# Moving operands of the down product and of block T3 placed in the uppermost 32 KB of the on-chip memory

## The chip, the cores and the metric

The kernel runs on one core of a Trainium2 chip. A core has a matrix engine (TensorE, PE in the profile; its weight loads are listed apart as PEld), three elementwise engines (VectorE or DVE, ScalarE or ACT, GpSimd or POOL), and a queue that only issues transfers (SyncE, SP). They share an on-chip memory of 128 partitions. Addresses below are in KB from the start of a partition, as the tiles get them when the two programs are built; the memory reaches to 224 KB, so "uppermost 32 KB" means 192 to 224. Matrix products are summed in a second memory, PSUM. The metric is the time of one execution on the device, in microseconds (us).

## The reference

One decoder layer on x of 1024 positions by 1024 columns, float32. Two token mixers (windowed attention and a chunked spatial gate) are merged by two gates and added to x; then follows a gated MLP with a causal width-3 convolution over positions:

```
x = x + (sigmoid(g_a) * (y_att @ w_oa) + sigmoid(g_b) * (y_sgu @ w_ob)) @ w_out
z = rmsnorm(x) @ w_up                    # 1024 x 1024 times 1024 x 5632
zc = conv_b + sum over 3 taps of conv_w[tap] * shifted z
x = x + (silu(gate half of zc) * value half) @ w_down     # 2816 x 1024
```

The change touches the gates (g_a, g_b are 2048 of the 3840 columns of a combined input projection), the up product and the down product.

## The kernel before

**Products.** Every float32 operand is split into a high and a low part (`copy_hi`, L75, on ScalarE, then a subtraction on GpSimd or VectorE), and a product is three matmuls: high by high, high by low, low by high. A matmul takes 128x128 weights and a moving operand of at most 512 columns, and each comes with its own weight load.

**Seven products for eight.** Gates, up product and down product use a scheme with seven block products on half-size blocks. On the side that moves, the blocks are named B11, T1, B21, B22, T2, T3, T4; on the weight side A11, A12, S1 to S4, A22. In the gates and the up product `Blocks.prod` (L914) issues 12 matmuls of 512 columns for one block product (4 blocks of the contraction, 3 each), so a pair of output tiles is 84 matmuls; there are 8 gate pairs (`first_gate_pair`, `gate_pair`) and 22 up pairs (`first_pair`, `fast_pair`). In both stages T3 is always multiplied with the weights s3h and s3l.

**The down product** (`mlp`) runs seven steps M1, M2, M6, M7, M4, M5, M3. Each is cut into six groups of 24 matmuls (the last: 12), 42 groups in all, numbered g = 0 to 41. The matmuls are those of L1595: weights ah, al, moving operands bh, bl. For a group `loads` fetches b (the stored activations) and the rows of w_down from DRAM, and `prep` makes ah, al, bh, bl in rings of four slots each: `copy_hi` for ah and bh on ScalarE, L1570 for al and bl (bl on GpSimd for g < 4, else on VectorE). `prep(g + 3)` is issued behind the matmuls of group g. b is held in three buffers.

**Order.** The order on the PE is written by hand. All transfers go through SP's queue in program order, and each engine does its instructions in order; waits come from the buffers: a tile placed where another one lay waits for the last use of that one. The last up pair still has its convolution, gating and stores to do when the down product begins: `q.gated()` and `q.stores()` stand behind group 1. `stores` writes five blocks to DRAM (`put`, L1338), two of them from the temporary tiles tt (L605). Only behind it is the pool of these temporaries closed and its space given to others.

**Homes of the tiles before.** Gates: T3 at 208 to 224, s3h and s3l at 203.5 to 207.5, other temporaries around them. Up product: T3 at 171.5 to 187.5, weights s3h and s3l at 165.5 to 169.5, and the pairs' temporaries (x1, x7, u2, tv, tg, tt) above, at 187.5 to 221.5. Down product: bh at 23.5 to 39.5, bl at 71.5 to 87.5, ah at 7.5 to 23.5, al at 87.5 to 103.5. Only two other sets of moving operands lie in the uppermost 32 KB for more than a few matmuls: wvB (the second half of an input weight, 208 to 225) and the attention keys.

**The twins wv and wvB.** In the projection for the spatial gate the same activations x are weights (at 23.5 to 103.5) for two moving operands of the same shape, 256 columns each: wv at 39.5 to 55.5 and wvB at 208 to 225. They take turns in one stretch, 192 matmuls each (L79 to L81).

Of the kernel before, what the change touches and what calls it, by code (L numbers as in the profile page):

```python
# [10 lines left out]
F = mybir.dt.float32  # L11
R = mybir.dt.float32r
# [29 lines left out]
def body(ctx, tc, nc, a):  # L42
# [7 lines left out]
    def nm(s):  # L50
        uid[0] += 1
        return f"{s}_{uid[0]}"

    def Y(s, dt=R, shape=None):
        return big.tile(shape or [128, 4, 1024], dt, tag="Y", name=nm(s), bufs=7)

    def U(s, dt=R, shape=None):

        return big.tile(shape or [128, 4, 1024], dt, tag="U", name=nm(s))
# [14 lines left out]
    def copy_hi(dst, src, scale=1.0):  # L74
        return nc.scalar.activation(dst, src, AF.Copy, scale=scale)  # L75
# [528 lines left out]
    def sub(eng, out, x, y, op=ALU.subtract):  # L604
        eng.tensor_tensor(out, x, y, op=op)  # L605
        return out
# [195 lines left out]
    pools = {"dr": dr}  # L802
# [31 lines left out]
    class Left:  # L834
# [54 lines left out]
                                                for x in "hl"))  # L889

        def split_s3(self):
            self.split(("S3",), self.s3, *(pools["wx"].tile([128, 4, 128], R, tag="s3" + x, name=nm("s3" + x))
                                           for x in "hl"))

        def split_r(self, n=0):
# [41 lines left out]
    def sums_load():  # L937

        i = sums["load"]
        if i < NPAIR:  # L940
            x = pools["ls"].tile([128, 3, 4, 128], F, tag="ls", name=nm("ls"), bufs=2)
            nc.sync.dma_start(x[:, 0], a["wup"][2 * i][:, 0:4])
            nc.sync.dma_start(x[:, 1:3], a["wup"][2 * i + 1].rearrange("p (b k) m -> p b k m", b=2))
            sums[i] = x
            sums["load"] += 1
# [25 lines left out]

    def gates_open():
        pools["ls_cm"] = tc.tile_pool(name="ls", bufs=1)
        pools["ls"] = pools["ls_cm"].__enter__()
        pools["gp_cm"] = tc.tile_pool(name="gp", bufs=1)
        gp = pools["gp"] = pools["wx"] = pools["gp_cm"].__enter__()
        pools["AX"] = gp.tile([128, 2, 1024], R, name="gax")
        sums_load()
# [174 lines left out]
    def open_out():  # L1153
        pools["mg_cm"].__exit__(None, None, None)
        pools["ls_cm"].__exit__(None, None, None)
        s3_cm.__exit__(None, None, None)
        pools["wx"] = ctx.enter_context(tc.tile_pool(name="wx", bufs=1, reuse_waits="tile"))
        pools["ex"] = ctx.enter_context(tc.tile_pool(name="ex", bufs=1, reuse_waits="tile"))
        pools["fp_cm"] = tc.tile_pool(name="fp", bufs=1, reuse_waits="tile")
        fp = pools["fp"] = pools["fp_cm"].__enter__()  # L1160
        for n in ("B11", "T1", "B21", "B22"):
            comb[n] = Y(n, R, [128, 2, 4, 512])
        comb["T3"] = pools["ex"].tile([128, 2, 4, 512], R, tag="T3", name="T3")
        pools["raw2"], pools["raw4"] = (fp.tile([128, 4, 512], F, name=n) for n in ("T2f", "T4f"))
        pools["sq2"] = fp.tile([128, 1024], F, name="sq2")
        dr = pools["dr"]
        pools["x2"] = [dr.tile([128, 1024], F, tag=f"x2_{d}", name=f"x2_{d}") for d in range(8)]
        for n in ("B11", "B21", "B22", "T1", "T2", "T3", "T4"):
            pools["d" + n] = [dr.tile([128, 512], F, tag=f"{n}_{i}", name=f"{n}_{i}") for i in range(HK)]
        out_load(D_ORDER[0])  # L1170
        psum["P"].insert(0, psum["P"].pop())
# [6 lines left out]
    def out_load(d):  # L1178
        acs[d] = pools["fp"].tile([128, 1024], F, tag="ac", name=nm("ac"), bufs=2)
        nc.sync.dma_start(acs[d], a["xw"][d, :, 257:1281])  # L1180
# [5 lines left out]
    def out_tile(i):  # L1186
        d = D_ORDER[i]

        def main(w):
            if i == 0:  # L1190
                open_out()
# [73 lines left out]
    late = {}  # L1265
# [219 lines left out]
        q.prod(q.g1, "S4", "B22", more=True)  # L1485
        return q

    SUM_AT = (2, 4, 5, 7, 8, 10)
    GR = [(k, min(k + 2, HK)) for k in range(0, HK, 2)]
    STEPS = ("M1", "M2", "M6", "M7", "M4", "M5", "M3")  # L1490
    RHS = {"M1": "B11", "M2": "B21", "M6": "T2", "M7": "T3", "M4": "T4", "M5": "T1", "M3": "B22"}
# [2 lines left out]
    def mlp():  # L1494
        groups = [(s, k0, k1) for s in STEPS for k0, k1 in GR]
        blk, ring = {}, {}
        zz = []

        def block(n, k0, k1):

            if k0 < 8:
                if n not in blk:
                    blk[n] = Y(n, F, [128, 8, 512])
                return blk[n][:, k0:k1, :]
            if not zz:
                zz.append(pools["ex"].tile([128, 8, 512], F, tag="T3", name="zz"))
            b = 3 * ("A11", "S2").index(n) - 8
            return zz[0][:, b + k0:b + k1, :]

        def slot(n, dt, cnt):  # L1510

            if n not in ring:
                y = pools["yd"].tile([128, 8, 512], F, name="rs") if n == "rs" else Y(n, dt, [128, 8, 512])
                ring[n] = [y, 0]
            y, i = ring[n]
            ring[n][1] += 1
            return y[:, 2 * (i % 4):2 * (i % 4) + cnt, :]
# [37 lines left out]
        def prep(g):  # L1555
            s, k0, k1 = groups[g]
            n = k1 - k0
            x, b = raw_.pop(g)
            if s == "M6":
                x = block("S2", k0, k1)  # L1560
            elif s in ("M7", "M3"):
                sub(nc.vector, x, x, block("S2", k0, k1))
            elif s == "M5":
                x = block("A11", k0, k1)
                sub(nc.vector, x, x, block("S2", k0, k1), ALU.add)
            out = []
            for t, nh, nl, eng in ((x, "ah", "al", nc.vector), (b, "bh", "bl", nc.gpsimd if g < 4 else nc.vector)):
                h, l = slot(nh, R, n), slot(nl, R, n)
                copy_hi(h, t)
                eng.tensor_tensor(l, t, h.bitcast(F), op=ALU.subtract)  # L1570
                out += [h, l]
            ops_[g] = out
# [26 lines left out]
        rs = {}  # L1599

        def res(n, t):

            r, c = int(n[1]) - 1, int(n[2]) - 1
            rs[n] = t
            for d in range(4):
                nc.sync.dma_start(t[:, d, :], pools["x2"][4 * r + d][:, 512 * c:512 * c + 512])
# [5 lines left out]
        def plus(n, d, p, last=False):  # L1612

            t = rs[n][:, d, :]
            nc.vector.scalar_tensor_tensor(t, p, 0.5, t, op0=ALU.mult, op1=ALU.add)
            if last:
                put(n, d, t)

        def done(s):
            for d in range(4):  # L1620
                if s == "M1":
                    nc.scalar.copy(Yb[d], X[d])
                if s == "M2":
                    plus("C11", d, Yb[d], True)
                if s == "M6":
                    plus("C21", d, X[d])
                if s == "M7":
                    nc.scalar.activation(rs["x7"][:, d, :], Yb[d], AF.Copy, scale=0.5)
                if s == "M4":
                    plus("C21", d, Yb[d], True)  # L1630
                if s == "M5":
                    plus("C22", d, X[d], True)
                if s == "M3":
                    plus("C12", d, X[d], True)
            if s == "M1":
                y = U("res", F, [128, 2, 4, 512])
                res("C11", y[:, 0])
                res("C21", y[:, 1])
                rs["y"] = y
            if s == "M2":  # L1640
                y = pools["yd"].tile([128, 2, 4, 512], F, name="res2")
                res("C22", y[:, 0])
                rs["x7"] = y[:, 1]
            if s == "M7":
                nc.vector.tensor_tensor(rs["C22"], rs["C22"], rs["x7"], op=ALU.add)
            if s == "M4":
                res("C12", rs["y"][:, 0])
# [18 lines left out]
        for g in range(len(groups)):  # L1666
            mms(g)
            s, k0, k1 = groups[g]
            while n_load < min(g + 6, len(groups)):
                loads(n_load)  # L1670
                n_load += 1
            if g in SUM_AT:
                sum_loads(*GR[SUM_AT.index(g)])
            if k1 == HK:
                done(s)
            if g == 0:
                q.tap_v()
                q.last_sum()
                q.conv_v()
                prep(2)  # L1680
                q.tap_g()
                q.conv_g()
            if g == 1:
                q.gated()
                q.stores()
                pools["ft_cm"].__exit__(None, None, None)
                pools["yd"] = ctx.enter_context(tc.tile_pool(name="yd", bufs=1, reuse_waits="tile"))
            if g + 3 < len(groups):
                prep(g + 3)
            if g - 2 in SUM_AT:  # L1690
                sums2(*GR[SUM_AT.index(g - 2)])
            if g == 0:
                q.tanh()
# [91 lines left out]
```

## Time and profile before

| | us |
|---|---|
| median of 3 runs | 1218.7 (1217.72 to 1218.85) |
| span of the profiled execution, first to last instruction | 1218.1 |
| PE busy in it | 1195.9 |
| DVE busy | 893.3 |
| ACT busy | 542.1 |
| POOL busy | 568.0 |

The page gives the profiled execution as its span of 1218.1; what lies around the span is the 0.6 between it and the median. A matmul's end is modelled in the trace, and neighbours overlap, so a mean duration of 389 ns says little: the pace of the PE is read from the distance of the starts.

### The profile page before, as it was taken

The numbers are of one execution on the slowest core, as the hardware profiler recorded it, in microseconds if no ns is written. First come the engines' busy times: TensorE is split into PE (matmuls) and PEld (weight loads), VectorE is DVE, ScalarE is ACT, GpSimd is POOL, SyncE is SP. The second block draws the span as 40 slices with busy tenths as digits, with TensorE's granted clock in tenths as the row PEclk, the third lists the DMA queues.
The fourth block names the chain that finished last, engine by engine and source line by source line (L and its number), as shares of the span: only waits on it lengthen the run. The fifth ranks groups of instructions, "written<-read, shape, count | busy, mean of one in ns | idle before, by whom it ended". The sixth has DMA issues, their size and how long they took to land.

```text
span 1218.1 us, 15838 instructions
## 1 busy us (share of the span) xinstructions
PE 1195.9 (98%) x5866; PEld 1004.7 (82%) x5866; DVE 893.3 (73%) x1033; ACT 542.1 (45%) x830; POOL 568.0 (47%) x358
## 2 busy tenths in 40 slices
PE   9999999889999999999999999999999999999998
PEld 8888889868887888888788888888888888888886
DVE  7788866874455665577798788887888888775674
ACT  8555566733434322223444444444444445424331
POOL 2466584278766522334756657566575642000000
PEclk9999999989999999999899999999999999999999
DMA  7010133125767897442223334233332347975471
GB/s 274 26 52 19 53 121 139 42 85 169 256 237 274 289 348 286 156 156 103 96 87 121 121 113 145 88 122 117 117 141 90 124 166 274 386 253 190 143 233 66
DMA packets 78989, 191.27 MB, mean 157 GB/s; under 512 B 8896, under 2 KB 9152, under 8 KB 78912
## 3 DMA queue, kind: packets, MB, share of 16 engines
q1 hardware_dynamic: 78912, 190.26, 44.3%
q8 instruction: 46, 0.75, 0.2%
q14 instruction: 31, 0.25, 0.1%
HBM read 139.63 MB, written 50.59 MB: 156 GB/s over the span
## 4 chain that ended last, share of the span: by engine, by line
PE 87%; DVE 6%; DMA 3%; ACT 2%; issue 1%; POOL 1%; SPq 0%; ACTq 0%; DVEq 0%
PE pz L914 42%; PE pd L1595 10%; PE pdy L1595 7%; PE px L81 2%; PE px L79 2%; PE po L79 2%; PE po L81 2%; PE po L80 2%; PE px L80 2%; DMA ls<-wup 2%; PE pv L498 1%; PE pu L81 1%; PE pu L79 1%; PE pu L80 1%; DVE T L750 1%; PE pq L79 1%
## 5 line engine op out<-in xcount | busy, mean ns | idle before, releaser
L914 PE MATMUL pz<-T,qh 128*128 128x512 f32 x464 | 142.8, 389 | 0.0
L879 POOL TENSOR_TENSOR pl<-lp,ph 128x1024 fp32r<-128x1024 f32 x30 | 73.6, 2455 | 85.0 <-ACT ph L75 84.9
L914 PE MATMUL pz<-B,ph 128*128 128x512 f32 x352 | 109.5, 392 | 0.0
L914 PEld LDWEIGHTS pz<-T,qh 128*128 128x128 f32 x464 | 87.2, 188 | 18.1
L914 PE MATMUL pz<-T,ql 128*128 128x512 f32 x232 | 90.3, 389 | 0.0
L96 POOL TENSOR_TENSOR wjl<-wj,wjh 128x512 fp32r<-128x512 f32 (+1 forms) x24 | 41.1, 1713 | 95.2 <-ACT wjh L75 95.2
L879 POOL TENSOR_TENSOR ql<-lq,qh 128x1024 fp32r<-128x1024 f32 x30 | 77.5, 2582 | 14.8 <-ACT qh L75 14.8
L914 PEld LDWEIGHTS pz<-B,ph 128*128 128x128 f32 x352 | 65.3, 188 | 15.5 <-ACT x L1443 1.9
L929 DVE TENSOR_TENSOR pz<-pz,rstd_b 128x1024 f32<-128x1024 f32 x60 | 73.9, 1232 | 3.0 <-ACT rstd_b L125 0.9
L879 POOL TENSOR_TENSOR s3l<-s,s3h 128x512 fp32r<-128x512 f32 x30 | 41.2, 1374 | 71.2 <-ACT s3h L75 67.0
L914 PE MATMUL pz<-T,s3h 128*128 128x512 f32 x232 | 71.7, 390 | 0.0
L914 PE MATMUL pz<-B,pl 128*128 128x512 f32 x176 | 68.6, 390 | 0.0
L1595 PE MATMUL pd<-bh,ah 128*128 128x512 f32 x176 | 68.5, 389 | 0.0
L1595 PE MATMUL pd<-bl,ah 128*128 128x512 f32 x176 | 68.5, 389 | 0.0
L1595 PE MATMUL pd<-bh,al 128*128 128x512 f32 x176 | 68.5, 389 | 0.0
L914 PE MATMUL pz<-T,AX 128*128 128x512 f32 x264 | 65.8, 400 | 0.0
L914 PE MATMUL pz<-B,AX 128*128 128x512 f32 x264 | 63.4, 389 | 0.0
L75 ACT ACTIVATE qh<-lq 128x1024 fp32r<-128x1024 f32 x30 | 31.9, 1063 | 66.7 <-issue 46.6
L914 PEld LDWEIGHTS pz<-T,AX 128*128 128x128 f32 x264 | 51.2, 194 | 10.8
L914 PEld LDWEIGHTS pz<-B,AX 128*128 128x128 f32 x264 | 49.6, 188 | 10.3
L1301 DVE SCALAR_TENSOR_TENSOR tg<-pz,cp,tg 128x1023 f32<-128x1023 f32 (+1 forms) x44 | 56.2, 1278 | 0.8
L1301 DVE SCALAR_TENSOR_TENSOR tv<-pz,cp,tv 128x1023 f32<-128x1023 f32 (+1 forms) x44 | 56.2, 1278 | 0.8
(333 smaller groups left out, 3556.9 us busy)
## 6 DMA issues: line engine op xcount, KB each, us to landing
ls<-wup SPq DMA_DIRECT2D x22, 512.0 KB, 5.9
sum<-ls SPq DMA_DIRECT2D x22, 512.0 KB, 5.3
lp<-wup SPq DMA_DIRECT2D x22, 512.0 KB, 3.6
ra<-wdown SPq DMA_DIRECT2D x44, 256.0 KB, 4.7
b<-T SPq DMA_DIRECT2D x44, 256.0 KB, 3.7
B<-tv SPq DMA_DIRECT2D x33, 256.0 KB, 2.0
T<-tt SPq DMA_DIRECT2D x33, 256.0 KB, 2.1
b<-B SPq DMA_DIRECT2D x33, 256.0 KB, 3.4
```

What stands on the lines that cost most here:

```text
L75: return nc.scalar.activation(dst, src, AF.Copy, scale=scale)
L79: nc.tensor.matmul(out, wh, mh, start=first, stop=False, **kw)
L80: nc.tensor.matmul(out, wh, ml, start=False, stop=False, **kw)
L81: nc.tensor.matmul(out, wl, mh, start=False, stop=last, **kw)
L96: nc.gpsimd.tensor_tensor(l[:, :nk, :], r[:, :nk, :], h[:, :nk, :].bitcast(F), op=ALU.subtract)
L498: nc.tensor.matmul(o, vhl[:, kb, g, :], w, start=i == 0, stop=i == len(ops) - 1)
L750: nc.vector.tensor_tensor(xb[n][:, 1, kk, :], src, xb[n][:, 0, kk, :].bitcast(F), op=ALU.subtract)
L879: nc.gpsimd.tensor_tensor(l, r, h.bitcast(F), op=ALU.subtract)
L914: nc.tensor.matmul(o, p[:, k, :], y[:, q, k, :], start=not more and k == 0 and j == 0, stop=k == 3 and j == 2, skip_group_check=True)
L929: nc.vector.tensor_tensor(z, z, rstd_b, op=ALU.mult)
L1301: nc.vector.scalar_tensor_tensor(t[:, j:], p[:, 0:1024 - j], cw[:, ci, 2 - j:3 - j], t[:, j:], op0=ALU.mult, op1=ALU.add)
L1595: nc.tensor.matmul(o[d], p[:, k - k0, m], q[:, k - k0, :], start=new and k == 0 and j == 0, stop=k == HK - 1 and j == 2, skip_group_check= ...
```

## The change

It gives tiles other addresses, and with these come other waits and one small move in a queue.

1. Gates: s3h and s3l are taken from the lower of two pools and lie at 177.5 to 181.5. T3 stays at 208 to 224. The weights gax move up by 4 KB to 193.5 to 201.5.
2. Up product: T3's pool is opened on the right side, so T3 lies at 208 to 224. Its weights stay at 165.5 to 169.5. The pairs' temporaries slide down by 16 KB (tt to 195.5 to 201.5, x1 to 201.5 to 205.5).
3. Down product: from group 4 on the parts of b go to two new rings, bh2 at 192 to 208 (it starts 32 bytes below 192 KB) and bl2 at 208 to 224; groups 0 to 3 keep the old ones. ah and al stay.
4. zz (a small block of operands), res and res2 (the residual) take homes that others left: zz at 119.5, res in bl's old place (71.5), res2 in bh's (23.5); rs (raw rows of w_down) lies at 171.5.
5. The first of six sums of w_down rows is loaded behind group 3 instead of group 2.

```diff
-            self.split(("S3",), self.s3, *(pools["wx"].tile(...
+            self.split(("S3",), self.s3, *(pools["s3w"].tile(...
...
-        pools["ls"] = pools["ls_cm"].__enter__()
+        pools["ls"] = pools["s3w"] = pools["ls_cm"].__enter__()
...
-        pools["wx"] = ctx.enter_context(tc.tile_pool(name="wx", bufs=1, reuse_waits="tile"))
-        pools["ex"] = ctx.enter_context(tc.tile_pool(name="ex", bufs=1, reuse_waits="tile"))
+        pools["wx"] = pools["s3w"] = ctx.enter_context(tc.tile_pool(name="wx", bufs=1, reuse_waits="tile"))
+        pools["ex_cm"] = tc.tile_pool(name="ex", bufs=1, side="right", reuse_waits="tile")
+        pools["ex"] = pools["ex_cm"].__enter__()
...
-    SUM_AT = (2, 4, 5, 7, 8, 10)
+    SUM_AT = (3, 4, 5, 7, 8, 10)
...
-                zz.append(pools["ex"].tile([128, 8, 512], F, tag="T3", name="zz"))
+                zz.append(U("zz", F, [128, 8, 512]))
...
-                y = pools["yd"].tile([128, 8, 512], F, name="rs") if n == "rs" else Y(n, dt, [128, 8, 512])
-                ring[n] = [y, 0]
+                p = pools["ydr"] if n in ("bh2", "bl2") else pools["yd"] if n == "rs" else None
+                ring[n] = [p.tile([128, 8, 512], dt, name=n) if p else Y(n, dt, [128, 8, 512]), 0]
...
-            for t, nh, nl, eng in ((x, "ah", "al", nc.vector), (b, "bh", "bl", nc.gpsimd if g < 4 else nc.vector)):
+            late = "2" if g > 3 else ""
+            for t, nh, nl, eng in ((x, "ah", "al", nc.vector),
+                                   (b, "bh" + late, "bl" + late, nc.gpsimd if g < 4 else nc.vector)):
...
-                y = U("res", F, [128, 2, 4, 512])
+                y = Y("res", F, [128, 2, 4, 512])
...
-                y = pools["yd"].tile([128, 2, 4, 512], F, name="res2")
+                y = Y("res2", F, [128, 2, 4, 512])
...
                 pools["ft_cm"].__exit__(None, None, None)
+                pools["ex_cm"].__exit__(None, None, None)
                 pools["yd"] = ctx.enter_context(tc.tile_pool(name="yd", bufs=1, reuse_waits="tile"))
+                pools["ydr"] = ctx.enter_context(tc.tile_pool(name="ydr", bufs=1, side="right", reuse_waits="tile"))
```

ScalarE, preparing groups 4 to 6 of the down product, with the semaphores that each instruction waits for (DMAHW0 to DMAHW7 count landed transfers, Pool is GpSimd). Before:

```order
L1321 ACTIVATE pz_8438<-tg_8638 128x1024 [waits DVE_49,Activation_49]
L75 ACTIVATE ah_8539<-zz 128x1024 [waits DMAHW7_49,DMAHW0_49,PE_49]
L75 ACTIVATE bh_8543<-b_8619 128x1024 [waits DMAHW5_49,DMAHW6_49,PE_49,Pool_49]
L75 ACTIVATE ah_8539<-zz 128x512 [waits DMAHW2_49,PE_49]
L75 ACTIVATE bh_8543<-b_8625 128x512 [waits DMAHW1_49,PE_49,Pool_49]
```

Now:

```order
L1322 ACTIVATE pz_8438<-tg_8638 128x1024 [waits DVE_49,Activation_49]
L75 ACTIVATE ah_8539<-zz_8622 128x1024 [waits DMAHW7_49,DMAHW0_49,PE_49]
L75 ACTIVATE bh_8699<-b_8619 128x1024 [waits DMAHW3_49,DMAHW5_49,DMAHW2_49,DMAHW6_49,DVE_49,Activation_49]
L75 ACTIVATE ah_8539<-zz_8622 128x512 [waits PE_49]
L75 ACTIVATE bh_8699<-b_8625 128x512 [waits DMAHW1_49]
```

bh_8699 is bh2, and b_8619 the third part of M1, for group 4. The order is the same, the waits are not: the copy into bh2 no longer waits for PE and GpSimd; besides the two transfers that bring b (DMAHW5, DMAHW6) it waits for two more, DMAHW2 and DMAHW3. These are the last two stores from tt, which lay where bh2 now lies.

SP's queue at the same place, from these stores on. Before:

```order
L1338 DMA T2_10_4867<-tt_1098_8683 128x512
L1338 DMA T4_10_4889<-tt_1099_8686 128x512
L1531 DMA b_1100_8721<-B21_2_4826 128x512
L1531 DMA b_1100_8721<-B21_3_4827 128x512
L1522 DMA ra_1097_8674<-wdown 128x512 x2
L1522 DMA S2_1101_8726<-wdown 128x512 x2
L1522 DMA rs_8727<-wdown 128x512 x2
L1531 DMA b_1102_8760<-B21_4_4828 128x512
L1531 DMA b_1102_8760<-B21_5_4829 128x512
L1522 DMA ra_1097_8674<-wdown 128x512 x2
```

Now:

```order
L1339 DMA T2_10_4867<-tt_1099_8683 128x512
L1339 DMA T4_10_4889<-tt_1100_8686 128x512
L1532 DMA b_1101_8727<-B21_2_4826 128x512
L1532 DMA b_1101_8727<-B21_3_4827 128x512
L1523 DMA ra_1098_8674<-wdown 128x512 x2
L1532 DMA b_1102_8760<-B21_4_4828 128x512
L1532 DMA b_1102_8760<-B21_5_4829 128x512
L1523 DMA ra_1098_8674<-wdown 128x512 x2
L1523 DMA S2_1103_8765<-wdown 128x512 x2
L1523 DMA rs_8766<-wdown 128x512 x2
```

The four loads into S2 and rs stand behind the loads of group 8 (b_1102 and ra) instead of ahead of them. Otherwise nothing changes places on any engine; the PE's matmuls come in the same order, with bh2 and bl2 for bh and bl from group 4 on.

## Rows read from the trace of the kernel before

**Rows 1.** The page, part 1: busy time of PE.

```profile
PE 1195.9 (98%) x5866; PEld 1004.7 (82%) x5866; DVE 893.3 (73%) x1033; ACT 542.1 (45%) x830; POOL 568.0 (47%) x358
```

**Rows 2.** Waits of the PE: who waited for whom, us in total, times, longest.

```profile
PE pe L914 <- DVE x L1012: 5.6, 1, 5.6
...
PE pz L1274 <- DVE sq L1394: 1.8, 1, 1.8
PE pz L914 <- ACT x L1034: 1.7, 1, 1.7
```

**Rows 3.** Windows, up and down product: busy by engine, clock, DMA share, GB/s.

```profile
700.00:1003.00 303.00, 303.00 (x1335) 249.69 (x1334) 251.07 (x241) 136.57 (x159) 181.25 (x92) 1.00 0.35 123
1003.00:1110.00 107.00, 107.00 (x474) 88.59 (x473) 83.99 (x81) 46.87 (x53) 8.16 (x4) 1.00 0.80 276
```

**Rows 4.** Timeline of PE, the twins: start, us, instruction, count.

```profile
186.36 0.28 PE L79 MATMUL pvs<-wv,x 128*128 128x256 f32 x1
...
189.23 0.29 PE L79 MATMUL pvs<-wvB,x 128*128 128x256 f32 x1
...
189.59 0.28 PE L79 MATMUL pvs<-wvB,x 128*128 128x256 f32 x1
...
191.97 0.28 PE L79 MATMUL pvs<-wvB,x 128*128 128x256 f32 x1
```

**Rows 5.** Timeline of PE, first gate pair: T1, then T3, then T2.

```profile
246.60 0.62 PE L914 MATMUL pe<-T,qh 128*128 128x512 f32 x2
...
249.32 0.63 PE L914 MATMUL pe<-T,s3h 128*128 128x512 f32 x2
...
252.12 3.10 PE L914 MATMUL pz<-T,gax 128*128 128x512 f32 x12
```

**Rows 6.** Timeline of PE, an up pair: T3, then B21.

```profile
796.46 0.61 PE L914 MATMUL pz<-T,s3h 128*128 128x512 f32 x2
...
799.17 0.67 PE L914 MATMUL pz<-B,ph 128*128 128x512 f32 x2
```

**Rows 7.** Matmuls of L1595, two of six forms: duration ns, first and last start.

```profile
L1595 PE MATMUL pd<-bh,ah x176: 389/389/389, 1003.7 to 1212.6; 128*128 128x512 f32 x176
...
L1595 PE MATMUL pdy<-bh,ah x132: 389/389/485, 1033.6 to 1152.7; 128*128 128x512 f32 x132
```

**Rows 8.** Timeline of PE: first matmuls of groups 4 and 6.

```profile
1025.45 0.39 PE L1595 MATMUL pd<-bh,ah 128*128 128x512 f32 x1
...
1033.61 0.39 PE L1595 MATMUL pdy<-bh,ah 128*128 128x512 f32 x1
```

**Rows 9.** Timeline of ACT and DVE: group 4's copy and subtraction.

```profile
1017.98 1.04 ACT L75 ACTIVATE bh<-b 128x1024 fp32r<-128x1024 f32 x1
...
1022.73 1.22 DVE L1570 TENSOR_TENSOR bl<-b,bh 128x1024 fp32r<-128x1024 f32 x1
```

**Rows 10.** Tile tt, 1015 to 1040 us: stores, time from issue to landing.

```profile
L1338 SPq DMA_DIRECT2D T<-tt x2: 394/790/1185, 1021.0 to 1021.7; - x2
...
DMA to landing us min/median/max: 4.1/4.2/4.2
```

**Rows 11.** The page, part 6: all 33 stores of this kind, KB each, median landing.

```profile
T<-tt SPq DMA_DIRECT2D x33, 256.0 KB, 2.1
```

**Rows 12.** Windows around three idle stretches of PE: PEclk third from the end.

```profile
222.00:232.00 10.00, 6.15 (x50) 5.74 (x50) 7.31 (x13) 6.78 (x13) 1.10 (x2) 1.00 0.00 0
254.00:261.00 7.00, 1.41 (x6) 0.88 (x6) 6.90 (x6) 0.00 (x0) 6.92 (x4) 0.71 0.00 0
261.00:264.00 3.00, 3.00 (x8) 2.41 (x9) 0.27 (x1) 0.00 (x0) 0.74 (x1) 0.53 0.25 76
```

**Rows 13.** Timeline of DVE, last but one gate pair.

```profile
377.58 4.13 DVE L605 TENSOR_TENSOR ls<-ls 128x512 f32<-128x512 f32 x2 [4.90 <-DMA ls<-wup]
```

**Rows 14.** Windows of the down product: the DMA share behind the stores.

```profile
1024.00:1034.00 10.00, 10.00 (x46) 8.29 (x45) 6.26 (x7) 3.74 (x6) 0.00 (x0) 1.00 0.85 295
1034.00:1044.00 10.00, 10.00 (x45) 8.29 (x45) 8.64 (x8) 4.57 (x6) 0.00 (x0) 1.00 1.05 390
```

More of the change, by code (lines that the diff above doesn't have):

```diff
@@ L891, in split_s3 @@
         def split_s3(self):
-            self.split(("S3",), self.s3, *(pools["wx"].tile([128, 4, 128], R, tag="s3" + x, name=nm("s3" + x))
+            self.split(("S3",), self.s3, *(pools["s3w"].tile([128, 4, 128], R, tag="s3" + x, name=nm("s3" + x))
                                            for x in "hl"))
```

## The prediction

> **What bounds the kernel now.** I read the page first: PE is busy for 1195.9 of 1218.1 us [rows 1]. Then the waits of the PE: the three longest that matter here sum to 9.1 us, and none lies behind the first up pair [rows 2]. Then windows by stage: from 700 us to 1110 us PE is busy all the time, beside DVE at 251 of 303 us in the up product [rows 3]. So in the up and the down product each nanosecond of a matmul's pace counts in full, and an edit that leaves the order of work alone can act in two ways only: through the pace, or through new waits.
>
> The pace is read in the timeline from the distance of the starts, by the place of the operands. From group 4 to group 6 of the down product there are 36 matmuls in 1033.61 - 1025.45 = 8.16 us, 226.7 ns each; moving operands and weights both lie below 192 KB [rows 8]. T3 of an up pair, at 171.5 KB, does 12 in 2.71 us, the same within the rounding of the starts [rows 6]. T3 of the first gate pair, at 208 KB with its weights at 203.5, needs (252.12 - 249.32)/12 = 233.3 ns; T1 just ahead, both operands below, 226.7 [rows 5]. And the twins at 256 columns: 24 matmuls with wv (39.5 KB) take 2.87 us, 119.6 each; with wvB (208 KB) and the same weights below, the 21 from the fourth on take 191.97 - 189.59 = 2.38 us, 113.3 each [rows 4].
>
> From 256 to 512 columns the pace below grows by 226.7 - 119.6 = 107.1 ns, which is 2.4 columns per ns, the full clock. Taking this for the streaming, a matmul costs over it 12.5 ns with both operands below (at either length), 6.2 with the moving one above and the weights below, and 19.1 with both above. The excess is one per matmul, not one per column: each has one weight load.
>
> **The change part by part.** Each sum is made against the profiled span of 1218.1; the median of the runs is 0.6 above it, and I add that at the end.
>
> The price of a 512-column matmul with its moving operand above and its weights below is in no row. From one side: streaming plus the excess of wvB, 214.2 + 6.2 = 220.4. If the whole pace of wvB scaled instead: 226.7 x 113.3/119.6 = 214.8. From the other side: 226.7 if nothing changes, and 233.3 if it is the place of T3 alone that costs in the gates. I take 220.4, since the excess below is the same 12.5 at 256 and 512 columns: 6.3 less than 226.7, 12.9 less than 233.3.
>
> Down product: 3 x (176 + 132) = 924 matmuls [rows 7], of which the 96 of groups 0 to 3 keep their place. 828 x 6.3 ns = 5.2 us off, all on the path [rows 3].
>
> Up product: 22 x 12 matmuls on T3. Those of the first pair lie ahead of a wait for VectorE (sq, 1.8 us [rows 2]) that takes up what they save. 252 x 6.3 = 1.6 us off. The temporaries' new places (tt and x1 share the upper part with T3) I cost at nothing: while wvB was read, ScalarE and VectorE worked on tiles at 201.5 to 205.5, and the pace was 113.3 [rows 4].
>
> Gates: 12 x 12.9 = 0.155 us a pair. The first pair's saving goes into the wait for VectorE (x L1012, 5.6 us [rows 2]). Those of the last two are lost in the wait for x L1034: there VectorE was held for 4.9 us by the transfer into ls [rows 13], and its late sums delay ScalarE's copy. Five pairs remain: 0.8 us off; ends 0 and 8 x 0.155 = 1.2. gax now lies wholly above as weights of operands below, as part of it did before; I cost this at nothing.
>
> The new wait. bh2's first copy, for group 4, waits until the two last stores from tt have landed. They are issued at 1021.0 and 1021.7 and land 4.1 and 4.2 us later, so at 1025.9 [rows 10]. Before, that copy ran at 1017.98 and the subtraction for bl at 1022.73 [rows 9], and group 4 began at 1025.45 [rows 8]. Now: copy 1025.9 to 1026.9 (1.04), subtraction to 1028.2 (1.22). The first matmul of group 4 waits 1.5 us, the second, which reads bl2 and would start at 1025.68, another 1.0: 2.5 us on. Bounds: with the median landing of such stores, 2.1 us [rows 11], it is 0.4; counted from the end of the longer issue (1.2 us more) 3.7. I take 2.5, from the stores themselves. What is queued behind it on ScalarE are the copies of groups 5 and 6; group 5 begins 24 x 0.2267 = 5.4 us after group 4, which is time for several copies of 1.04. On SP the loads of b for group 7 wait for the buffer that group 4's subtraction frees, 4.2 us later than before. The DMA engines are full from 1034 us on [rows 14], but the change takes 1 MB (the four loads into S2 and rs, 2.7 us at 390 GB/s) out from ahead of group 8's loads, and group 7 begins only 5.4 us after group 6, at 1039.0 + 2.5: nothing. If that cover failed, it would be a second, smaller stall of up to 2 us.
>
> The rest: zz, res, res2 and rs lie on tiles whose last use is groups earlier, and ac's first load in the output projection waits for VectorE and ScalarE, which are ahead of it in any case. A wait that stayed hidden there costs nothing; none of the PE's waits is in that stage now [rows 2].
>
> Sum: 5.2 + 1.6 + 0.8 - 2.5 = 5.1 off. 1218.1 - 5.1 = 1213.0 in the span, 1213.6 in the median.
>
> **Rivals.** First, that a weight load never slows a matmul, so place does nothing for the pace. The Trainium skill says so (TensorE: Matmul & The Clock Gate, Step-by-step: what each phase is for): the engine has one memory port for the moving operand and one for weights, and loading the next weights takes nothing from the running matmul. The twins speak against the rule, with 119.6 and 113.3 on the same weights [rows 4]. As a mechanism of this kernel: the savings are 0 and the wait of 2.5 remains: 1221.2. For it speaks that no row has 512 columns above with weights below. Chance 8%.
>
> Second, the slower one: at 512 columns the upper part is slow for whatever streams from it, as T3 in the gates was [rows 5]; only short operands gain. Then 828 + 252 matmuls cost 6.6 more, 7.1 us, the gates stay, and with the wait it is 9.6 on: 1228.3. It decides from a pace of about 226.7 on, where the wait alone is left. Against it: the weights were above as well in the gates. Chance 6%.
>
> Third, the saving scales with the columns (214.8): 828 x 11.9 = 9.9, 252 x 11.9 = 3.0, 60 x 18.5 = 1.1, less 2.5: 1207.2. Against it, the equal excess of 12.5 below. Chance 12%.
>
> Fourth, the stall lowers the clock. Where PE idled for 5.6 us [rows 2], the clock then fell to half: 0.71 over 7 us and 0.53 over 3 [rows 12], together 6.9 us at 1.2 GHz, which is 3.4 us of work lost. Two idle stretches that left PE 3.85 us short in ten, with matmuls between them, left it at 1.00 [rows 12], and mine is 1.5 and 1.0. If it falls: 1213.6 + 3.4 = 1217.0. Chance 12%.
>
> **How the numbers follow.** My forecast has 62%. Its own range is 1211 (stall 0.4, gates 1.2) to 1215 (stall 3.7). With the third and fourth the range that I give is 1207 to 1217.5, which leaves out the first two and a little more. A run can tell 0.2%, 2.4 us, from no change. Faster by more: forecast and third, 74%, and a point for a milder fall of the clock: 0.75. Within 0.2%: the fourth, and half of the first, whose 2.5 lies at the bound: 0.16. Slower: 0.09.
>
> **What would show it.** In the timeline of PE, starts about 220 apart in T3 of the gates, of the up product and from group 4 of the down product on, and 227 in T1 and in groups 0 to 3. Among PE's waits, one or two new ones at L1595 (its new line) at group 4, some 2.5 us together, with ScalarE's copy into bh2 released by the stores from tt. Clock 1.00 behind it. I am wrong if the pace stays at 226.7 or goes to 233, if the new wait is missing or has followers at groups 7 to 9, or if the clock falls behind it.

## The result, and the profile after

| | before | after |
|---|---|---|
| median of 4 runs each on one chip, us | 1218.21 (1216.55 to 1218.85) | 1230.58 (1227.44 to 1231.72) |
| ratio, 95% interval | | 1.0098 (1.0076 to 1.0120) |
| span of the profiled execution, us | 1218.1 | 1229.1 |

The changed kernel is 12.4 us slower by the medians (their quotient, 1.0102, lies inside the interval); 1213.6 was forecast. One of its four runs took 1227.44 at a mean granted clock of 0.996, the other three 1230.2 to 1231.7 at 0.991 or 0.992. On the page, PE's busy time grows by 10.6 us, that of its weight loads (PEld) by 3.4 and that of the other engines by at most 0.9 [rows 1]:

```profile
PE 1206.5 (98%) x5866; PEld 1008.1 (82%) x5866; DVE 894.2 (73%) x1033; ACT 542.8 (44%) x830; POOL 567.8 (46%) x358
```

First the pace. The timeline of PE in the changed kernel, T3 of the first gate pair up to T2, then T3 of an up pair up to B21 (columns as in [rows 5, 6]):

```profile
250.08 0.63 PE L914 MATMUL pe<-T,s3h 128*128 128x512 f32 x2
...
252.88 0.39 PE L914 MATMUL pz<-T,gax 128*128 128x512 f32 x1
...
796.36 0.63 PE L914 MATMUL pz<-T,s3h 128*128 128x512 f32 x2
...
799.16 0.39 PE L914 MATMUL pz<-B,ph 128*128 128x512 f32 x1
```

Both take 2.80 us for 12 matmuls, 233.3 ns each. In the gates that is what it was [rows 5], though the weights now lie at 177.5 KB; in the up product it was 2.71 us [rows 6]. In the down product I take the same 300 matmuls of both kernels, well behind group 6. Windows, before:

```profile
1107.50:1175.63 68.13, 68.13 (x301) 56.19 (x300) 42.64 (x42) 27.40 (x32) 0.00 (x0) 1.00 0.57 188
```

And after:

```profile
1115.42:1185.54 70.12, 70.12 (x301) 56.09 (x300) 42.91 (x42) 27.38 (x32) 0.00 (x0) 1.00 0.56 184
```

227.1 against 233.7 ns each, with the clock at 1.00, DVE, ACT and the transfers as busy as before. So wherever a 512-column operand came from the upper part, the pace was 233, not 220.

Second, the new wait. PE's waits in the changed kernel:

```profile
PE pd L1598 <- ACT bh L75: 2.2, 1, 2.2
PE pz L1275 <- DVE sq L1395: 1.7, 1, 1.7
PE pd L1598 <- DVE bl L1573: 0.8, 1, 0.8
```

The two at L1598 are new; the wait for x at L1034 [rows 2] is missing in this execution. ScalarE's copy into bh2, and what released it:

```profile
1027.19 1.06 ACT L75 ACTIVATE bh<-b 128x1024 fp32r<-128x1024 f32 x1 [8.64 <-DMA T<-tt]
```

PE at the start of group 4 and behind it:

```profile
1025.74 0.39 PE L1598 MATMUL pd<-bh,al 128*128 128x512 f32 x1
1028.30 0.50 PE L1598 MATMUL pd<-bh,ah 128*128 128x512 f32 x1 [2.17 <-ACT bh L75]
1029.56 0.50 PE L1598 MATMUL pd<-bl,ah 128*128 128x512 f32 x1 [0.76 <-DVE bl L1573]
1029.90 0.39 PE L1598 MATMUL pd<-bh,al 128*128 128x512 f32 x1
...
1031.38 0.63 PE L1598 MATMUL pd<-bl,ah 128*128 128x512 f32 x1
1031.81 0.63 PE L1598 MATMUL pd<-bh,al 128*128 128x512 f32 x1
```

The starts are 2.56 and 1.26 us apart where 0.23 would do: 2.3 + 1.0 = 3.4 us lost, with 2.5 forecast. Then the distance is 0.43 for eight matmuls. Windows of that stretch and of what follows (PEclk third from the end):

```profile
1030.90:1034.00 3.10, 3.10 (x9) 2.36 (x8) 2.08 (x2) 0.29 (x1) 0.00 (x0) 0.50 1.05 295
1034.00:1110.00 76.00, 76.00 (x327) 61.25 (x326) 54.38 (x53) 30.58 (x34) 0.00 (x0) 1.00 0.84 295
```

The granted clock was 0.50, that is 1.2 of 2.4 GHz, for 3.1 us behind two idle stretches of 2.2 and 0.8 us, and 1.00 after: 8 x (0.427 - 0.234) = 1.5 us more.

The books: 828 x 6.7 ns = 5.5 in the down product, 264 x 6.6 = 1.7 in the up product, 3.4 for the wait, 1.5 for the clock: 12.1, beside the 12.4 us between the medians. The two profiled spans are only 11.0 apart, since the wait at L1034 (1.7 us before) is missing from the second.

### The profile page after: what moved, and what is told of

It is laid out like the page before. It is cut to its first block, busy times and chain, and to the rows that moved or that the text cites. A ratio compares the mean times of both kernels' runs of the same rounds, so it can differ in the third digit from the quotient of the medians.

```text
span 1229.1 us, 15834 instructions
## 1 busy us (share of the span) xinstructions
PE 1206.5 (98%) x5866; PEld 1008.1 (82%) x5866; DVE 894.2 (73%) x1033; ACT 542.8 (44%) x830; POOL 567.8 (46%) x358
## 4 chain that ended last, share of the span: by engine, by line
PE 87%; DVE 6%; ACT 3%; DMA 2%; issue 1%; POOL 1%; SPq 0%; ACTq 0%; DVEq 0%
PE pz L914 44%; PE pd L1598 8%; PE pdy L1598 8%; PE px L80 2%; PE po L81 2%; PE po L80 2%; PE px L79 2%; PE px L81 2%; PE po L79 2%; PE pv L498 1%; PE pu L81 1%; PE pu L79 1%; PE pu L80 1%; DVE T L750 1%; PE pq L79 1%
## 5 line engine op out<-in xcount | busy, mean ns | idle before, releaser
L1598 PE MATMUL pd<-bh,ah 128*128 128x512 f32 x176 | 70.1, 398 | 2.2 <-ACT bh L75 2.2
L1598 PE MATMUL pd<-bl,ah 128*128 128x512 f32 x176 | 69.9, 397 | 0.8 <-DVE bl L1573 0.8
L1598 PE MATMUL pd<-bh,al 128*128 128x512 f32 x176 | 69.9, 397 | 0.0
```

The lines of the kernel that those rows point to most:

```text
L1598: nc.tensor.matmul(o[d], p[:, k - k0, m], q[:, k - k0, :], start=new and k == 0 and j == 0, stop=k == HK - 1 and j == 2, skip_group_check= ...
```

## The experiments

Theory A, as the result suggests: the upper part streams a 512-column operand more slowly. Its rivals came with the runs.

**m1_sweep: matmuls alone.** It computes none of the layer: 1034 matmuls in order, sixteen to a case, the moving operand at `m`, the weights at `w`.

```
for cols in (128, 192, 256, 320, 384, 448, 512):
    mms(cols, M_LOW, W_LOW); mms(cols, M_TOP, W_LOW); mms(cols, M_LOW, W_TOP); mms(cols, M_TOP, W_TOP)
for cols in (512, 256):
    for kb in SWEEP: mms(cols, kb * KB, W_LOW, step=0)      # twelve addresses, 12 to 202 KB
```

> This kernel computes nothing of the layer: 1034 matmuls in a fixed order, sixteen to a case, with weights at 120 or 204 KB and the moving operand at 40 or 194 KB, for 128 to 512 columns, then one moving operand at twelve addresses from 12 to 202 KB, then other weight addresses, the same weights again and again, and VectorE and ScalarE busy on tiles below or above. Theory A, the upper part streams each column more slowly but spares the cost per matmul: moving operands below cost about 13.3 ns + 0.4167 ns a column (113 to 120 ns at 256, 227 at 512), above about 0.47 ns a column less 7 (53 at 128, 113 at 256, 233 at 512), whatever the weights' place; the two lines cross near 390 columns, and the address sweep steps once, near 192 KB. Theory B, the upper part is slower only while other engines work on tiles there: without traffic 512 columns take about 220 to 227 above as well, and 233 or more only in the last case. Theory C, the weights' place counts: above with above 233, above with below 220 at 512. Theory D, the twins differed by something other than place: 256 columns take the same above and below.

Windows of single cases (the count at PEld is the number of weight loads, one per matmul, give or take one at the edges): 256 columns from 40 and from 194 KB, 512 columns from 40 and from 194 KB, then 512 columns from all twelve addresses.

```profile
43.76:45.70 1.94, 1.94 (x19) 1.94 (x17) 0.00 (x0) 0.00 (x0) 0.00 (x0) 1.00 0.00 0
45.70:47.62 1.92, 1.92 (x19) 1.92 (x17) 0.00 (x0) 0.00 (x0) 0.00 (x0) 1.00 0.00 0
85.16:88.84 3.68, 3.68 (x18) 3.00 (x16) 0.00 (x0) 0.00 (x0) 0.00 (x0) 1.00 0.00 0
88.84:92.46 3.62, 3.62 (x17) 3.00 (x16) 0.00 (x0) 0.00 (x0) 0.00 (x0) 1.00 0.00 0
99.72:143.24 43.52, 43.52 (x194) 36.06 (x192) 0.00 (x0) 0.00 (x0) 0.00 (x0) 1.00 0.00 0
```

3.62/16 = 226.3 and 43.52/192 = 226.7 ns: above or below, nothing changes at 512 columns, and nothing at 256 (120). The third line, 3.68 or 230 ns from 40 KB, is the first case behind another length, and such a case reads a little apart; the same operand at 40 KB with weights at 150 KB reads 226.7. The cases with VectorE and ScalarE busy on tiles below or above read 226.6 to 226.8 as well. Neither A nor B, C survives as it stands; D does. What the sweep had equalized unawares is the start: all its operands began on a multiple of 512 bytes.

**e1, e2, e3: the change in parts.** Edits, against before (e1) and against the changed kernel (e2, e3):

```diff
e1  -pools["ex"] = ctx.enter_context(tc.tile_pool(name="ex", bufs=1, reuse_waits="tile"))
    +pools["ex_cm"] = tc.tile_pool(name="ex", bufs=1, side="right", reuse_waits="tile")
e2  -pools["ex_cm"] = tc.tile_pool(name="ex", bufs=1, side="right", reuse_waits="tile")
    +pools["ex_cm"] = tc.tile_pool(name="ex", bufs=1, reuse_waits="tile")
    -...pools["s3w"].tile([128, 4, 128], R, tag="s3" + x, ...
    +...pools["wx"].tile([128, 4, 128], R, tag="s3" + x, ...
e3  -late = "2" if g > 3 else ""
    +late = "2" if g > 5 else ""
```

> The kernel before, with T3 of the up product alone moved to 208 to 224 KB (its weights stay at 165.5), gates and down product as they were. If the place of a 512-column moving operand costs 6.6 ns a matmul (A), T3 of every up pair goes from 226.7 to 233.3, 264 x 6.6 = 1.7 us on: about 1219.9, ratio 1.0014. If 220.4 held without the traffic of tiles slid down beside it (B), the pace would be 233 here too, as the temporaries are where the changed kernel has them: the two differ in the sweep, not here. If the up product had nothing to do with the loss: 1218.2. No new wait at the down product, so no stall and no fall of the clock.

> The changed kernel with T3 of the up product back at 171.5 KB and the gates' weights back at 203.5: what is left are the down product's rings above. A: pace 233 to 234 from group 4 on, 828 x 6.6 = 5.5 us on, the stall of about 3 us and, if it lowers the clock again, 2 us more: about 1227 to 1229. If the up product's T3 carried the loss: under 1224. T3 of the up product is back at 226.7; T3 of the gates stays at 233, since its own place has not changed.

> The changed kernel with the new rings used from group 6 on instead of group 4, so that the stores from tt have landed when the first copy into bh2 is due; 780 instead of 828 matmuls read from above. If the stall and the clock's fall behind it cost what the starts say (2.6 + 0.8 us at groups 4 and 5, 8 matmuls at 427 ns: 1.7 us), and the pace the rest: about 1230.6 - 3.4 - 1.7 - 0.3 = 1225. If the time behind the stall would be taken up by another wait, 1229 or more. The matmuls before the copy's place keep 226.7, those behind 233 to 234.

| | median us | ratio to before (15 runs, 1217.66) |
|---|---|---|
| e1 (11 runs) | 1219.44 | 1.0015 (1.0006 to 1.0023) |
| e2 (5) | 1226.32 | 1.0069 (1.0055 to 1.0083) |
| e3 (5) | 1225.01 | 1.0059 (1.0046 to 1.0071) |

e1 costs the 1.7 us of its pace. T3 of the up pair:

```profile
794.12 0.63 PE L914 MATMUL pz<-T,s3h 128*128 128x512 f32 x2
...
796.92 0.39 PE L914 MATMUL pz<-B,ph 128*128 128x512 f32 x1
```

e3 has no wait at L1598 and no fall of the clock, and its 300 matmuls are as slow as those of the changed kernel:

```profile
1108.82:1178.92 70.10, 70.10 (x302) 56.23 (x301) 42.55 (x42) 27.40 (x32) 0.00 (x0) 1.00 0.56 183
```

So the stall with the clock is worth about 1230.6 - 1225.0 - 0.3 (48 matmuls) = 5.3 us, near the 4.9 read in the trace, and the pace is the rest. By the two ratios, each against runs of before beside it, it is 4.4. In e2 (1226.3, with 1227 to 1229 expected) the temporaries lie 16 KB higher, so that tt lies under bl2 and not under bh2, ScalarE's copy waits for a store from tv, and the stall cost less: waits at L1598 of 0.4 and 0.9 at group 4 and of 0.7 at group 6, and the clock stayed at 1.00. All three bear out the sizes, and say nothing yet on why 233.

**m2_align: the start of the operands.** Again matmuls alone. The moving operand's start (`o`) and the weights' (`wo`) are given in bytes past a multiple of 512.

```
for o in range(0, 512, 32): mms(cols, M_LOW + off(o), W_LOW + off(32))
for mo in (32, 480):
    for wo in (0, 32, 64, 96, 128, 256, 480): mms(512, M_LOW + off(mo), W_LOW + off(wo))
```

> This kernel computes nothing of the layer: matmuls in a fixed order, sixteen to a case. In the first sweep the place had no effect at all (226.7 at 512 columns and 120.0 at 256, above and below), and all its operands began on a multiple of 512 bytes. In the kernels, the tiles below 192 KB begin 32 bytes behind such a multiple, those from the right end 32 bytes ahead of one (480). Theory E, the start of the moving operand within 512 bytes sets the pace, wherever it lies: 32 as 0 (226.7 and 120.0), 480 gives 233.3 at 512 columns and 113.3 at 256, in the lower part too, and the same offset reads alike at 194 KB and at 40 KB; the weights' offset changes nothing. Theory B, the place counts only beside the work of other engines: every offset 226.7 and 120.0. Theory F, the offset of the weights against that of the moving operand counts: the pace changes in the rows with other weights as well.

Six cases of 512 columns: 32 and 480 at 40 KB, 32 and 480 at 194 KB, all with weights at 32; then 480 at 40 KB with weights at 32 and at 480.

```profile
33.33:36.99 3.66, 3.66 (x18) 3.01 (x17) 0.00 (x0) 0.00 (x0) 0.00 (x0) 1.00 0.00 0
85.29:89.02 3.73, 3.73 (x18) 3.02 (x17) 0.00 (x0) 0.00 (x0) 0.00 (x0) 1.00 0.00 0
122.92:126.55 3.63, 3.63 (x17) 3.01 (x16) 0.00 (x0) 0.00 (x0) 0.00 (x0) 1.00 0.00 0
137.69:141.43 3.74, 3.74 (x18) 3.01 (x16) 0.00 (x0) 0.00 (x0) 0.00 (x0) 1.00 0.00 0
205.04:208.77 3.73, 3.73 (x17) 3.01 (x16) 0.00 (x0) 0.00 (x0) 0.00 (x0) 1.00 0.00 0
223.71:227.34 3.63, 3.63 (x17) 3.01 (x16) 0.00 (x0) 0.00 (x0) 0.00 (x0) 1.00 0.00 0
```

Read the second and the fourth line first: 480 gives 3.73 to 3.74 us (233) below and above alike. The last two lines have the same moving operand; only the weights moved, from 32 to 480, and 3.73 fell to 3.63 (226.9). So it is not the start of the moving operand that counts (E), but how it stands to the weights' (F). Of the sixteen starts against weights at 32, only 32 and 288 gave 228 and 227, which is a period of 256 bytes; 96 and 352 gave 229, the others 233 to 234. Starts off a multiple of 32 (4, 8, 16 and 48 bytes) gave 231 to 237.

That sorts the rows of before. Tiles allotted from the left begin 32 bytes past a multiple of 256, those from the right 224 past it: the difference is 192 for wvB, for T3 of the gates whichever pool holds its weights, and now for T3 of the up product, bh2 and bl2.

**m3_places: place against offset.** Eight places from 40 to 204 KB for each of four differences. An excerpt:

```
for d in (0, 64, 128, 192):
    for kb in (40, 72, 104, 140, 170, 194, 200, 204): mms(cols, kb * KB + off(32 + d), W_LOW + off(32))
```

> This kernel computes nothing of the layer: matmuls in a fixed order, sixteen to a case, the moving operand at eight places from 40 to 204 KB with its offset 0, 64, 128 or 192 bytes past that of the weights (120 KB), at 512 and at 256 columns. Theory F at 512 columns: 226.7, 229, 233.3, 233.3, alike at all eight places. At 256 columns the second sweep read 113.6 below and 117.8 above for the same 192: if the place matters there, the three places above read 117.8 and the five below 113.6 again; if it was the order of the cases, all eight read alike. Theory A: a step between 170 and 194 KB at 512 columns.

Windows of 128 matmuls, all eight places together: 512 columns with a difference of 0, 64, 128 and 192 bytes, then 256 columns with 0 and with 192.

```profile
29.60:58.64 29.04, 29.04 (x130) 24.03 (x128) 0.00 (x0) 0.00 (x0) 0.00 (x0) 1.00 0.00 1
58.64:87.95 29.31, 29.31 (x129) 24.04 (x128) 0.00 (x0) 0.00 (x0) 0.00 (x0) 1.00 0.00 1
87.95:117.69 29.74, 29.74 (x129) 24.12 (x128) 0.00 (x0) 0.00 (x0) 0.00 (x0) 1.00 0.00 1
117.69:147.57 29.88, 29.88 (x130) 23.94 (x129) 0.00 (x0) 0.00 (x0) 0.00 (x0) 1.00 0.00 1
147.57:162.91 15.34, 15.34 (x129) 15.34 (x128) 0.00 (x0) 0.00 (x0) 0.00 (x0) 1.00 0.00 1
193.17:207.58 14.41, 14.41 (x130) 14.41 (x128) 0.00 (x0) 0.03 (x1) 0.00 (x0) 1.00 0.00 1
```

Divided by 128: 226.9, 229.0, 232.3 and 233.4 ns at 512 columns; at 256 columns 119.8 and, over the 127 distances of the last window, 113.5. The first place of each case, behind another case, reads up to 1.6 ns apart; the other seven agree within 0.9. So a difference of 192 costs some 6.5 ns at 512 columns and gives back as much at 256. This is F. The 117.8 that m2 read at 194 KB for 256 columns and the same 192 did not come back here, so the place does not make it; that the order of the cases made it is not shown, and the cause stays open.

**e4, e5: offsets made equal, places kept.** The changed kernel (e4) and e3 (e5) with 192 bytes of padding:

```diff
+ts = [pools["s3w"].tile([128, 560 - 32 * (x == "l")], R, tag="s3" + x, ...) for x in "hl"]
+... t[:, n:n + 512] ... for t, n in zip(ts, (48, 0))       # s3h, s3l start 192 bytes later
+pools["pad"].tile([128, 48], F, name="pad")                # bh2, bl2 start 192 bytes earlier
```

> The changed kernel, every operand above as it is, but with 192 bytes of padding: s3h and s3l start 192 bytes later in gates and up product, bh2 and bl2 192 bytes earlier, so that moving operand and weights of every 512-column matmul start on the same offset within 256 bytes. The sweeps read 226.7 ns where the two offsets are equal and 233 where they differ by 192, above and below. Theory F (the difference of the two offsets sets the pace): T3 of gates and up product and the down product from group 4 on go back to 226.7 though they stay above 192 KB: 264 x 6.6 + 828 x 6.8 + some 0.5 in the gates = 7.8 us off the changed kernel's 1230.6, about 1222.8; the stall at group 4 and the fall of the clock behind it stay. Theory A (the place above 192 KB sets the pace in the kernel, beside other engines' work, whatever a kernel of matmuls alone shows): 233 and 1230.6 as before.

> The same padding in the version whose new rings begin with group 6 (1225.0, no stall). Theory F: 264 x 6.6 + 780 x 6.8 + 0.5 = 7.5 us off, about 1217.5, within 0.1% of the kernel before: with offset and stall gone nothing of the loss is left, and the upper part gives nothing either. Theory A: 1225. If a further cost were hidden behind the pace (SP's order, the residual's new home): 1219 or more.

| | median us | ratio to before (29 runs, 1217.34) |
|---|---|---|
| e4 (6 runs) | 1222.55 | 1.0052 (1.0038 to 1.0066) |
| e5 (12) | 1218.20 | 1.0009 (0.9996 to 1.0021) |

T3 of an up pair in e4, at 208 KB, 2.73 us for 12, and the 300 matmuls of the down product:

```profile
794.60 0.62 PE L916 MATMUL pz<-T,s3h 128*128 128x512 f32 x2
...
797.33 0.39 PE L916 MATMUL pz<-B,ph 128*128 128x512 f32 x1
```

```profile
1110.09:1178.28 68.19, 68.19 (x302) 56.23 (x300) 42.64 (x42) 27.40 (x32) 0.00 (x0) 1.00 0.57 186
```

227.5 and 227.3 ns with the moving operands above 192 KB. e4 keeps the stall, without a fall of the clock, and with a follower at group 6. PE's waits and the window behind the stall:

```profile
PE pd L1600 <- ACT bh L75: 1.7, 1, 1.7
...
PE pdy L1600 <- ACT pdy L1627: 1.0, 1, 1.0
...
PE pd L1600 <- DVE bl L1575: 0.8, 1, 0.8
```

```profile
1028.00:1031.00 3.00, 3.00 (x15) 2.45 (x14) 2.21 (x2) 0.42 (x1) 0.00 (x0) 1.00 0.84 285
```

The follower begins on SP. Its load of b waits for the late subtraction of group 4 (5.4 us, before 1.0), the rows of w_down (ra) behind it land late, ScalarE waits for them, and its copy of M1's sums (pdy), to which group 6 adds, stands behind that:

```profile
SPq L1534 <- DVE bl L1575: 5.4, 1, 5.4
```

```profile
1032.91 1.06 ACT L75 ACTIVATE ah<-ra 128x1024 fp32r<-128x1024 f32 x1 [4.50 <-DMA ra<-wdown]
1033.88 1.04 ACT L75 ACTIVATE bh<-b 128x1024 fp32r<-128x1024 f32 x1
1034.83 2.27 ACT L1627 COPY pdy<-pd 128x512 f32<-128x512 f32 x4
```

In e5, without the stall, no difference from before is left that these runs can tell. Within the 0.2% that the interval leaves, offset and stall, with the clock behind it, are the whole loss, and the uppermost 32 KB give nothing by themselves.

**e7: the same loss below.** The kernel before, T3 of the up product 192 bytes higher, at 171.7 KB.

```diff
-comb["T3"] = pools["ex"].tile([128, 2, 4, 512], R, tag="T3", name="T3")
+t3 = pools["ex"].tile([128, 4160], R, tag="T3", name="T3")
+comb["T3"] = t3[:, 48:4144].rearrange("p (a b c) -> p a b c", a=2, b=4)
```

> The kernel before, with T3 of the up product 192 bytes higher (171.7 KB instead of 171.5), far below 192 KB; nothing else changes but the temporaries behind it, by 256 bytes. Theory F: 233.3 in T3 of every up pair, 264 x 6.6 = 1.7 us on, about 1219.9, ratio 1.0014, the same loss as T3 in the upper part gave (1.0015). Theory A: 226.7, no change.

Measured: 1218.90 (12 runs), ratio 1.0019 (1.0007 to 1.0031); T3 again 2.80 us for 12:

```profile
797.19 0.63 PE L914 MATMUL pz<-T,s3h 128*128 128x512 f32 x2
...
799.99 0.39 PE L914 MATMUL pz<-B,ph 128*128 128x512 f32 x1
```

**e8: the twins.** The kernel before, the tile of wvB and of the gates' T3 starting 192 bytes earlier, still at 208 KB (one run):

```diff
-wv.append(zr[0].tile([128, 2, 8, 256], R, tag="Z", name="wvB"))
+z = zr[0].tile([128, 4144], R, tag="Z", name="wvB")
+wv.append(z[:, 0:0 + 4096].rearrange("p (a b c) -> p a b c", a=2, b=8))
```

> The kernel before, with the tile that holds wvB and later T3 of the gates starting 192 bytes earlier, still at 208 KB, so that both have the same offset as their weights (x, s3h, s3l). Theory F: wvB loses its advantage, 113.3 to 120 ns like its twin wv, and T3 of the gates gains, 233.3 to 226.7, both in the upper part as before; the time hardly moves (192 x 6.4 = 1.2 us on at most, 96 x 6.6 = 0.6 off). Theory A: wvB stays at 113.3 and T3 at 233.3, as neither leaves its place.

wvB, 48 matmuls in a row, first and last; T3 of the first gate pair up to T2:

```profile
189.76 0.28 PE L79 MATMUL pvs<-wvB,x 128*128 128x256 f32 x1
...
195.40 0.28 PE L81 MATMUL pvs<-wvB,x 128*128 128x256 f32 x1
...
251.93 0.62 PE L915 MATMUL pe<-T,s3h 128*128 128x512 f32 x2
...
254.65 0.39 PE L915 MATMUL pz<-T,gax 128*128 128x512 f32 x1
```

wvB takes 5.64/47 = 120.0 ns, as wv does, and T3 2.72/12 = 226.7: both changed as F has it, without leaving the upper part. The one run took 1219.5, before beside it 1217.95; single runs of before lie from 1213.8 to 1219.8, so this says nothing about the time.

**e6: offsets chosen by length.** The kernel before; T3 of the gates equal to its weights, and the first half of wq and wv 192 bytes past x:

```diff
+y = big.tile([128, 4160 if i == "2" else 4096], dt, tag="Y" + i, name=nm(s))
+n = 48 if i == "2" and s in ("wq", "wv") else 0
```

> The kernel before, with the offsets chosen by length: T3 of the gates starts 192 bytes earlier (equal to s3h and s3l), while the first half of wq and wv, moving operands of 256 columns with x as weights, start 192 bytes later, as wvB does against x. Everything stays where it was otherwise; the homes that the ring of seven gave are written out. Theory F with the twins' numbers: 384 x 6.4 = 2.4 us off in the projections, and 60 to 96 x 6.6 = 0.4 to 0.6 in the gates: about 1215.2, ratio 0.9975. If the attention around wq is held by other engines, 1216.4. Theory A: wv and wq stay at 120 as they lie below: 1218.2.

Measured: 1217.14 (12 runs), ratio 1.0001 (0.9988 to 1.0014). The forecast 0.9975 lies outside. The pace moved in part: T3 of the gates went to 226.7 and wv from about 120 to 113 or 114 (its first two groups of 24 to 118), but the first half of wq, forecast at 113, only from 121 to 124 down to 116 to 123. The time did not move. One place may show where the gain of wv went, PE's wait for ScalarE in the spatial gate, 3.9 us in the profile of before:

```profile
PE pm L87 <- ACT pm L818: 4.9, 2, 2.8
```

That is 1.0 us more, and wv's saving, 192 x (119.5 - 114.2) ns by the starts, is 1.0. But in the other kernels' profiles this wait reads 2.9 to 3.9, and the profiled execution was the slowest of the twelve, so this is not shown. For wq and the gates, where other waits vary by 1 to 2 us from run to run, it is not settled either. No version faster than the kernel before was found.

## Why the prediction was wrong

**The step that failed** is "the price of a 512-column matmul with its moving operand above and its weights below", taken as 220.4 ns from "streaming plus the excess of wvB". It is 233.3 to 233.7. The prediction had read the difference of the twins as one of place, carried it over to 512 columns as one excess per matmul, and laid T3's 233.3 in the gates to weights that lay above too. The runs put one cause behind all of these rows: the starts of moving operand and weights modulo 256 bytes (m2, m3, e4, e7, e8). The difference of 192 that saves some 6.5 ns at 256 columns costs as much at 512, so no carrying over from the shorter length could have given even the sign. Nor was the equal excess of 12.5 at both lengths, the reason given for 220.4, evidence for it: the streaming had been taken as the difference of the two paces, so the two excesses are equal by the subtraction. In m1, with equal starts, what a matmul takes above 2.4 columns per ns is 13.3 ns at 256, 320, 384 and 512 columns, but 20.0 at 448 (206.7), so it is not one cost per matmul either. The rows were read rightly; the label on them, "above", was one that they could not tell from "allotted from the right".

**Its three terms.** Down product: -5.2 forecast, +5.5 measured. Up product: -1.6, and +1.7. Gates: -0.8, and nothing, since moving the weights from 203.5 to 177.5 KB left the difference of the starts at 192.

**The wait.** The mechanism held: the copy into bh2 waits for the stores from tt, then subtraction and PE. The size was 3.4 for 2.5, in the main since the stores landed 4.8 us after their issue instead of the 4.2 of [rows 10]; that it comes near the named upper bound of 3.7, which counted from the end of a longer issue, is chance. The two stores in the changed kernel:

```profile
DMA to landing us min/median/max: 4.8/4.8/4.8
```

The follower, "a second, smaller stall of up to 2 us", came in e2 and e4 (0.7 and 1.0 us). It is the one that the prediction named and priced at nothing: SP's load of b behind the late subtraction. It struck one group earlier than looked for, at group 6, because the copy of M1's sums stands behind group 7's copies on ScalarE. In the changed kernel's profile it is missing: PE came to group 6 only at 1039.36 us, when ScalarE's copy had begun at 1037.98.

**The rivals.** The second, slower one had the place and the pace right (233.3, 1228.3 with the wait); its reason, a slow upper part, is refuted by m1, m3 and e4. The fourth happened on top: in the profiled execution the clock fell to half behind the stall and cost 1.5 of the 3.4 us allowed. Together 1228.3 + 1.5 + 0.9 (the longer wait) = 1230.7. What spoke against it, a clock of 1.00 around two idle stretches [rows 12], did not decide. PE idles at that same place in both kernels, for 1.74 and 2.11 us before and 1.75 and 2.11 after, and right behind it the clock stayed up in the one profile and fell in the other. Before, then after:

```profile
232.00:236.00 4.00, 4.00 (x35) 4.00 (x34) 3.87 (x7) 3.20 (x4) 0.00 (x0) 1.00 0.02 4
```

```profile
232.00:236.00 4.00, 4.00 (x23) 4.00 (x23) 3.57 (x6) 3.20 (x4) 0.00 (x0) 0.58 0.02 4
```

So the length of such waits alone did not settle whether the clock fell, and how often it falls behind the new stall is open: one execution was profiled. The first rival, the old pace and the wait alone (1221.2), fell 9.4 us short. In m2 a shift of the weights alone moved the pace from 233.1 to 226.9. The rule named beside this rival, that loading the next weights takes no memory bandwidth from the running matmul (the Trainium skill, TensorE: Matmul & The Clock Gate, Step-by-step: what each phase is for), does not by itself lead one to expect that.

**The chances.** All that spoke of the pace hung on one comparison in which place, pool side and start changed together. A bound from 233.3 stood in the text, at 6%; nothing in the rows made it less likely than 220.4.

## What to carry to other kernels

Where a run of matmuls is bound by PE, compare the start addresses of weights and moving operand modulo 256 bytes: at 512 columns keep them equal (226.7 ns here, up to 237 otherwise), at 256 columns a difference of 192 was the fastest (113 against 120). Other lengths need rows of their own: at 448 columns, in m2, equal starts were the slowest of five (206 ns, a difference of 64 gave 200). Before a difference between two tiles is laid to where they are, list everything else in which their addresses differ, and carry it to another length only with a row at that length. A tile placed where stores read from waits until they have landed, so begin using the new home some groups later (e3 and e5 lost nothing by it).

## What was not expected of the hardware

- The pace of float32 matmuls on split operands depends on the starts of weights and moving operand relative to each other, with a period of 256 bytes (m2, m3): at 512 columns 226.7 ns at 0, 229 at 64, 232 at 128, 233.3 at 192; at 256 columns 119.8, 117.8, 118.6 and 113.3; at 128, 192 and 320 columns the starts tried made no difference but in the first case behind another length (111.7, 111.7 and 146.7). In the sweeps each matmul has its own weight load, as in the kernels. The weights alone were moved at 512 columns only, and why the starts count no run shows.
- The address itself, from 12 to 204 KB, does not matter at 512 and 256 columns (m1, m3), nor, at 512 columns with equal starts, the work of VectorE and ScalarE on other tiles (226.6 to 226.8 in m1).
- Two idle stretches of 2.2 and 0.8 us with one matmul between them were followed by 3.1 us at half clock. Stretches of nearly the same length at one place of the program, 1.74 and 2.11 us and 1.75 and 2.11 us, were followed by a clock of 1.00 in one execution and 0.58 over four us in another.
